# mLSTM scores and sums as three rounded products, with the values' remainders in DRAM

## The chip, the cores and the metric

The kernel runs on one core of one Trainium2 chip. The metric is the time of one execution in microseconds (us) on the device. Its engines are named as in the profile: PE is TensorE (PEld its weight loads), DVE VectorE, ACT ScalarE, POOL GpSimd, SP SyncE, which issues most of the DMAs.

## The reference

One decoder layer on 512 tokens of width 1024, in float32. An mLSTM with four heads (queries and keys of 128, values of 256) and a windowed attention run beside each other on one normalised input; sigmoid gates merge them; an output projection, a squared-ReLU MLP and a gated embedding follow.

```python
qk_ml = jax.nn.silu(causal_depthwise_conv(qk_ml, conv_qk[i]))
q_ml, k_ml = jnp.split(qk_ml, 2, axis=-1)
...
# mLSTM, chunkwise; over the whole sequence a head computes
scores = jnp.einsum("bhtk,bhsk->bhts", qc, kc) * jnp.exp(log_d - m_t[..., None])
num = (... + jnp.einsum("bhts,bhsv->bhtv", scores, vc))
den = ... + jnp.sum(scores, axis=-1)
h = num / jnp.maximum(jnp.abs(den), jnp.exp(-m_t))[..., None]
...
y_a = jax.nn.sigmoid(o_ml) * h_ml          # h_ml: h normalised per head
y_b = swa_with_sinks(...)                  # the local branch
merged = jax.nn.sigmoid(g_a) * (y_a @ w_branch_a[i]) + jax.nn.sigmoid(g_b) * (y_b @ w_branch_b[i])
x = x + merged @ w_out[i]
u = rmsnorm(x, norm_mlp_g[i]) @ w_up[i]
x = x + jnp.square(jax.nn.relu(u)) @ w_down[i]
```

## The kernel before, in words

All 512 tokens stay on the chip. A projection is made of rounded products: each float32 operand is split (`split`) into a high part, rounded to the type fp32r by a ScalarE copy, and a low part, what VectorE's subtraction leaves of it. `pairs` names the three products high x high, high x low and low x high, which `chain` adds up in one PSUM bank. Weights go through `load_w`: SP loads 512 KB into a `wr` tile, ScalarE casts it to `wh`, VectorE makes `wl`. `split_by_transfer` makes a low part in another way: ScalarE writes the negated high part, and an accumulating DMA from POOL's queue adds the source (its rows are at L147).

The stages that the change touches come in this order. First `by_tokens(w_vml, ...)`: the values, with `seven`, which forms the product of two 2 x 2 block matrices from seven block products, named p1, c11, t21, t22, c22, c12 and c21 after what becomes of them. The function `post` takes each from PSUM: p1 is copied, the t are p1 plus a product, and the c go to `put_v`, which writes a token tile of values `vm[m]` (all heads, 257 columns each, the last one ones, so that the sums over scores come out of the same matmul). Then the mLSTM's gates, rows of 4 x 512 (`mst`, the running maximum; `rr`; `gg`; `em`), TensorE's transposes of gg and em, and `by_tokens(w_o, ...)`, the output gate, with its own p1 to c21. Then the gates of the branches, the conv, and the local branch's attention.

Last comes the stage of the heads. `ml_decay(h)` makes a head's decay weights with ten exps into four tiles `dm`. `ml_scores(h)` multiplies keys and queries (float32 matmuls, four blocks, the causal part alone) and VectorE multiplies the decay in. `ml_out(h)` sums them over values: ten float32 matmuls in two PSUM tiles. `ml_norm` normalises, `branch_b(i)` is one of eight projections of the local branch (24 products of 512 columns), `ya_of(h)` transposes a head's result and splits it into the two big tiles `ya`, and `merge` projects those.

The order of instructions on each engine isn't that of the program text: a scheduler places them ahead of time by its own estimate of durations, and `issue_after` gives it limits. Tiles come from pools of numbered buffers, and a new tile waits until the last reader of the buffer's tile before it is through. The pool `act` has `NACT` = 34 buffers of 128 x 512, and nearly every short-lived tile lives in it; `lm` has four buffers of 128 x 1024, `big` two of 8 x 512 columns. PSUM has two buffers each of `psg` and `pst` (one bank) and of `psa` (two banks).

Of the kernel before, what the change touches and what calls it, by code (L numbers as in the profile page):

```python
# [22 lines left out]
NEG = -1e30  # L23
NH = 4
DV = 256
# [7 lines left out]
LMB = 4  # L33
# [3 lines left out]
def block_kernel(  # L37
# [29 lines left out]
    nc = tc.nc  # L67
    V, A, G, T = nc.vector, nc.scalar, nc.gpsimd, nc.tensor
# [18 lines left out]
    def nm(s):  # L87
        n_names[0] += 1
        return f"{s}_{n_names[0]}"
# [16 lines left out]
    def act_f(n="f"):  # L106
        return ap.tile([P, 512], F32, tag="act", bufs=NACT, name=nm(n))

    def act_r(n="r"):
        return ap.tile([P, 512], F32R, tag="act", bufs=NACT, name=nm(n))  # L110
# [4 lines left out]
    def big_hl(n):  # L115

        hl = [bp.tile([P, KT, 512], F32R, tag="big", bufs=2, name=nm(n)) for _ in range(2)]
        return hl, [[t[:, k, :] for t in hl] for k in range(KT)]

    def tk(n):  # L120
        return tp_.tile([P, NH * (DV + 1)], F32, tag="tk", bufs=4, name=nm(n))

    def tok_scratch(n="lm"):
        return sp.tile([P, D], F32, tag="lm", bufs=LMB, name=nm(n))
# [4 lines left out]
    def r32(t):  # L129
        return t.bitcast(F32)  # L130
# [3 lines left out]
    def split(dst, src, scale=None):  # L134

        if scale is None:
            A.copy(dst[0], src)  # L137
            last_low[0] = V.tensor_sub(dst[1], src, r32(dst[0]))  # L138
        else:
            A.activation(dst[0], src, AF.Copy, scale=scale)  # L140
            V.scalar_tensor_tensor(dst[1], src, scale, r32(dst[0]), ALU.mult, ALU.subtract)
# [21 lines left out]
    def pairs(a, b):  # L163

        return [(a[0], b[0]), (a[0], b[1]), (a[1], b[0])]

    last_mm = [None]
# [36 lines left out]
    ones = cp.tile([P, P], F32, name="ones")  # L204
# [129 lines left out]
    on_scalar, _ = columns(0, xn)  # L334
# [4 lines left out]
    _, on_vector = columns(1, xn)  # L339
    for m in range(NT):  # L340
        if m == 1:
            with tc.issue_after(on_vector):
                xn, _ = norm(2)
# [17 lines left out]
    dp = pool(ctx, "dp", space=bass.MemoryType.DRAM)  # L361
# [3 lines left out]
    with tc.issue_after(gate_in.ins):  # L365
        hi, lo = [r32(t[:, :, :P]) for t in h2]
# [37 lines left out]
    for i in range(2):  # L404
        ps = proj_T(w_ksw, i, ps_t)
        both = [act_r("kk"), act_r("kk")]
        low = [act_r("kl"), act_r("kl")]
        for ab in range(2):
            s, o = HALF[ab], HALF[1 - ab]
# [67 lines left out]

    vm = []
    for m in range(NT):
        t = tk("vm").rearrange("p (h d) -> p h d", h=NH)  # L480
        G.memset(t[:, :, DV : DV + 1], 1.0)
        vm.append(t)

    def by_tokens(w, post, own_first=False):

# [30 lines left out]

    def put_v(m, nh, ps, k):
        o = vm[m][:, 2 * nh : 2 * nh + 2, :DV]
        src = ps.rearrange("p (h d) -> p h d", h=2)
        if k is None:  # L520
            A.copy(o, src)
        else:
            V.tensor_add(o, src, k.rearrange("p (h d) -> p h d", h=2))

    pg = ps_a()
    pgi, pgf = pg[:, :512], pg[:, 512:]
# [134 lines left out]
    qk = [None] * 8  # L661
# [113 lines left out]
    for h in range(NH):  # L775
        silu(h)
        silu(4 + h)


    hs = [[act_f("hs") for _ in range(2)] for _ in range(NH)]  # L780
    hd = c1.tile([P, NH, NT], F32, name="hd")
    hss = c1.tile([P, NH, NT], F32, name="hss")
    wts = {}
# [4 lines left out]
    def ml_decay(h):  # L788
        pr = rows[h]
        dg = act_f("dg")  # L790
        V.tensor_tensor(
            dg.rearrange("p (t j) -> p t j", t=NT),
            pr.rearrange("p (t j) -> p t j", t=NT),
            tri.unsqueeze(1).broadcast_to([P, NT, P]),
            ALU.add,
        )
        wT = []
        for s in range(NT):
            dm = act_f("dm")
            for t in range(s, NT):  # L800
                src = dg if t == s else pr
                A.activation(
                    dm[:, t * P : (t + 1) * P],
                    src[:, t * P : (t + 1) * P],
                    AF.Exp,
                    bias=gc[:, t * NT + s, h : h + 1],
                )
            wT.append(dm)
        wts[h] = wT

    def ml_scores(h):

        two, one = ps_a(), ps_t()
        banks = [two[:, :512], two[:, 512:], one, two[:, 512:]]
        at = [0, 0, 0, 384]
        for s in (0, 1, 3, 2):
            n0 = s * P
            psc = banks[s][:, at[s] : at[s] + S - n0]
            T.matmul(psc, qk[4 + h][:, n0 : n0 + P], qk[h][:, n0:], start=True, stop=True, skip_group_check=True)  # L819
        for s in range(NT):  # L820
            n0 = s * P
            dm = wts[h][s]
            V.tensor_mul(dm[:, n0:], banks[s][:, at[s] : at[s] + S - n0], dm[:, n0:])

    def ml_out(h):
        wT = wts.pop(h)
        for half in (1, 0):
            pn = ps_a().rearrange("p (n c) -> p n c", n=2)
            for t in (2 * half, 2 * half + 1):
                for s in range(t + 1):  # L830
                    last_mm[0] = T.matmul(  # L831
                        pn[:, t % 2, : DV + 1], wT[s][:, t * P : (t + 1) * P], vm[s][:, h, :], start=s == 0, stop=s == t, skip_group_check=True
                    )
            A.copy(hs[h][half].rearrange("p (n c) -> p n c", n=2), pn[:, :, :DV])
            V.tensor_copy(hd[:, h, 2 * half : 2 * half + 2], pn[:, :, DV])
        den = small("den", NT, 2)
        V.scalar_tensor_tensor(den, hd[:, h, :], -1.0, hd[:, h, :], ALU.mult, ALU.max)
        V.tensor_max(den, den, gc[:, NT * NT :, h])
        rd = small("rd", NT, 3)
        V.reciprocal(rd, den)  # L840
        jk = act_f("jk")
        for t in range(NT):
            A.activation(jk[:, :DV], h_of(h, t), AF.Square, scale=rd[:, t : t + 1], accum_out=hss[:, h, t : t + 1])
        return rd
# [15 lines left out]
    def branch_b(i):  # L860
        ps = ps_g()
        mm_T(ps, load_w(w_b[i], KT * P, KT), yb)
        t2[i] = act_f("gb")
        V.tensor_mul(t2[i], ps, gate_of(gbd, i))


    _, ya = big_hl("ya")

    def ya_of(h):
        for i in (2 * h, 2 * h + 1):  # L870
            pt = ps_t()
# [2 lines left out]
            split(ya[i], pt, gml[:, i : i + 1])  # L874

    ml_decay(0)
    ml_scores(0)
    rds = []
    for h in range(NH):
        branch_b(h)  # L880
        if h + 1 < NH:
            ml_decay(h + 1)
        with tc.issue_after(last_mm[0].ins):
            rds.append(ml_out(h))
        if h + 1 < NH:
            with tc.issue_after(last_mm[0].ins):
                ml_scores(h + 1)
        if h == 1:
            ml_norm([0, 1], rds)
        elif h > 1:  # L890
            ml_norm([h], rds[h:])
    for h in range(NH):
        branch_b(NH + h)
        ya_of(h)


    F11, F12, F22, G1, G2, G3, G4 = ([] for _ in range(7))

# [96 lines left out]
    _, x1 = big_hl("x1")  # L995
# [273 lines left out]
    def one(n):  # L1269
        return tp.tile([P, 1], F32, tag=n, bufs=4, name=nm(n))  # L1270
# [48 lines left out]
    for m in range(NT):  # L1319
        for o, n in ((0, 512),) if m == 0 else ((0, 256), (256, 256)):  # L1320
            ps = ps_g()[:, :n]
# [4 lines left out]
            if o == 0:  # L1326
                s = one("fse")
# [102 lines left out]
```

## Time and profile before

| what | value |
|---|---|
| median of 3 runs (lowest to highest) | 881.58 us (881.02 to 881.89) |
| the profiled execution's own time | 881.1 us |
| its span | 879.3 us |
| busy: PE, DVE, ACT, POOL | 99%, 75%, 55%, 3% |
| mean granted clock of TensorE | 0.997 |
| DMA moved | 105.16 MB, 120 GB/s |
| stage of the values, first to last product | about 47 to 82 us |
| output gate | about 83 to 126 us |
| stage of the heads, first projection of the local branch to the first merge | 325.4 to 399.5 us |

The span is the time that the profile covers; 1.8 us of the profiled execution's time lie outside it. Rows of the timeline give the start and the duration of an instruction in us; matmuls are pipelined, so the distance from one start to the next says what a matmul takes, not its duration. A float32 matmul shows as two records.

### The profile page before, as it was taken

To read this page: it belongs to the slowest core of one execution; us is meant where nothing else is said; L and a number is where in the kernel's file an instruction comes from. 1 tells how busy PE (TensorE), PEld (TensorE's weight loads), DVE (VectorE), ACT (ScalarE), POOL (GpSimd) and SP (SyncE) were. 2 spreads that over 40 slices of the span, in tenths; PEclk is the share of its full clock that TensorE was granted. 3 is DMA by queue.
4 is the path that set the end of the run, shared out by engine and by line. 5 is a ranking of instruction groups with operands and counts; after the bars stand their busy time and mean duration, and the time that the engine had idled before them with its cause. 6 is when DMAs were issued, how large, how long until landed. Compare 5 with 4: busy or idle time off the path is not lost.

```text
span 879.3 us, 11531 instructions
## 1 busy us (share of the span) xinstructions
PE 866.8 (99%) x4372; PEld 725.4 (82%) x4372; DVE 661.1 (75%) x972; ACT 481.0 (55%) x799; POOL 28.8 (3%) x52
## 2 busy tenths in 40 slices
PE   8999999999999999999999999999999999999996
PEld 7888889998777777888888888888888888887886
DVE  6999887875789876665896669757956784699557
ACT  6684554544675768743344665356435534544843
POOL 1111010000000000000020000000000000000000
PEclk9999999999999999999999999999999999999998
DMA  7765244435122162364244612530452054102402
GB/s 266 211 188 176 73 152 165 166 115 195 49 73 72 49 202 85 99 238 144 72 82 148 226 48 72 203 108 2 140 172 72 1 191 144 48 25 75 142 0 96
DMA packets 31929, 105.16 MB, mean 120 GB/s; under 512 B 4477, under 2 KB 4477, under 8 KB 31874
## 3 DMA queue, kind: packets, MB, share of 16 engines
q1 hardware_dynamic: 27570, 93.15, 30.6%
q0 software_dynamic: 4160, 11.02, 4.8%
q8 instruction: 34, 0.56, 0.3%
q10 hardware_dynamic: 144, 0.26, 0.1%
q14 instruction: 21, 0.17, 0.1%
HBM read 91.30 MB, written 8.40 MB: 113 GB/s over the span
## 4 chain that ended last, share of the span: by engine, by line
PE 89%; DVE 4%; ACT 3%; DMA 2%; issue 1%; SPq 0%; ACTq 0%; DVEq 0%
PE psg L171 49%; PE psp L171 23%; PE psa L171 7%; PE pst L171 4%; PE psa L831 1%; PE pst L747 1%; DVE wl L138 1%; DMA wr<-in_w_vsif 1%; ACT lm L712 1%; PE psa L819 1%; PE psa L689 1%; PE psa L690 1%; ACT wh L137 0%; DMA wr<-in_w_gb 0%; PE psp L980 0%
## 5 line engine op out<-in xcount | busy, mean ns | idle before, releaser
L137 ACT CAST wh<-wr 128x1024 fp32r<-128x1024 f32 x138 | 144.8, 1052 | 181.6 <-PE psg L171 71.7
L138 DVE TENSOR_TENSOR wl<-wr,wh 128x1024 fp32r<-128x1024 f32 x138 | 167.6, 1220 | 83.7 <-ACT wh L137 82.5
L171 PE MATMUL psg<-x,wh 128*128 128x512 f32 x512 | 157.7, 389 | 0.0
L171 PE MATMUL psp<-wh,uf 128*128 128x512 f32 x448 | 138.6, 389 | 0.0
L171 PEld LDWEIGHTS psg<-x,wh 128*128 128x128 f32 x512 | 96.0, 188 | 19.9
L171 PE MATMUL psg<-x,wl 128*128 128x512 f32 x256 | 99.6, 389 | 0.0
L171 PEld LDWEIGHTS psp<-wh,uf 128*128 128x128 f32 x448 | 84.1, 188 | 17.4
L171 PE MATMUL psp<-wl,uf 128*128 128x512 f32 x224 | 87.3, 390 | 0.8 <-DVE wl L138 0.8
L171 PE MATMUL psg<-h,wh 128*128 128x512 f32 x256 | 81.1, 395 | 0.7 <-DVE rc L715 0.7
L137 ACT CAST wh<-wd 128x1024 fp32r<-128x1024 f32 x44 | 46.2, 1053 | 56.4 <-PE psp L171 21.9
L138 DVE TENSOR_TENSOR wl<-wd,wh 128x1024 fp32r<-128x1024 f32 x44 | 53.2, 1220 | 14.6 <-ACT wh L137 14.5
L171 PEld LDWEIGHTS psg<-x,wl 128*128 128x128 f32 x256 | 48.0, 188 | 10.0
L171 PEld LDWEIGHTS psg<-h,wh 128*128 128x128 f32 x256 | 47.0, 188 | 11.2 <-issue 1.6
L171 PE MATMUL psg<-h,wl 128*128 128x512 f32 x128 | 50.5, 395 | 0.0
L171 PEld LDWEIGHTS psp<-wl,uf 128*128 128x128 f32 x224 | 42.0, 188 | 10.0 <-DVE wl L138 1.2
L138 DVE TENSOR_TENSOR uf<-F,uf 128x1792 fp32r<-128x1792 f32 (+2 forms) x20 | 33.0, 1652 | 21.8 <-ACT uf L137 21.8
L171 PE MATMUL psg<-yb,wh 128*128 128x512 f32 x128 | 41.3, 402 | 0.1
L171 PE MATMUL psg<-ya,wh 128*128 128x512 f32 x128 | 39.5, 390 | 0.0
L137 ACT CAST uf<-F 128x1792 fp32r<-128x1792 f32 (+2 forms) x20 | 27.9, 1396 | 20.6 <-DVE F L1133 20.4
L1157 DVE SCALAR_TENSOR_TENSOR xk<-psp,r,xk 128x512 f32<-128x512 f32 x48 | 33.8, 745 | 4.9 <-PE psp L171 4.7
L171 PE MATMUL psa<-h,wh 128*128 128x256 f32 x192 | 35.3, 285 | 0.3 <-ACT p L625 0.3
L171 PE MATMUL psg<-hS,wh 128*128 128x256 f32 x192 | 35.6, 284 | 0.0
(321 smaller groups left out, 1742.1 us busy)
## 6 DMA issues: line engine op xcount, KB each, us to landing
wr<-in_w_up SPq DMA_DIRECT2D x32, 512.0 KB, 3.2
wd<-in_w_down SPq DMA_DIRECT2D x24, 512.0 KB, 3.6
wr<-in_w_qsw SPq DMA_DIRECT2D x8, 512.0 KB, 3.7
gd<-gr POOLq DMA_DIRECT2D x8, 512.0 KB, 3.5
wr<-in_w_qkml SPq DMA_DIRECT2D x8, 512.0 KB, 3.2
wr<-in_w_b SPq DMA_DIRECT2D x8, 512.0 KB, 3.2
gl<-gd SPq DMA_DIRECT2D x8, 512.0 KB, 3.2
wr<-in_w_a SPq DMA_DIRECT2D x8, 512.0 KB, 4.1
```

The costliest lines, as they stand in the source:

```text
L137: A.copy(dst[0], src)
L138: last_low[0] = V.tensor_sub(dst[1], src, r32(dst[0]))
L171: last_mm[0] = T.matmul(ps, l, r, start=first and i == 0, stop=last and i == len(ops) - 1, skip_group_check=parts)
L689: T.matmul(o, q[:, n * P : (n + 1) * P], kk[kp][ab][:, k0 : k0 + 256], start=True, stop=False)
L690: T.matmul(o, q[:, n * P : (n + 1) * P], kl[kp][ab][:, k0 : k0 + 256], start=False, stop=True)
L712: A.activation(lm3[:, g, :], lm3[:, g, :], AF.Exp, bias=nmx[:, g : g + 1], scale=0.125, accum_out=sm[:, g : g + 1])
L747: T.matmul(o[HALF[ab], :], v[:, c : c + 64], w[:, ab * 512 : (ab + 1) * 512], start=j == 0, stop=j == len(terms) - 1)
L819: T.matmul(psc, qk[4 + h][:, n0 : n0 + P], qk[h][:, n0:], start=True, stop=True, skip_group_check=True)
L831: last_mm[0] = T.matmul(pn[:, t % 2, : DV + 1], wT[s][:, t * P : (t + 1) * P], vm[s][:, h, :], start=s == 0, stop=s == t, skip_group_check ...
L1157: pin(V.scalar_tensor_tensor(o, ps[:, t, :], r2[:, 2 * toks + t : 2 * toks + t + 1], o, ALU.mult, ALU.add))
```

## The change

What it does:

- `put_v` keeps the values' high parts in `vm` (now fp32r, 258 columns a head, the last two ones, written by ScalarE in place of POOL's memset) and makes a remainder `vl` of each of eight half tiles: two by VectorE's subtraction, six by a negated copy on ScalarE and an accumulating DMA. POOL stores all eight in DRAM (`vld`).
- `ml_out` reads a head's remainders back (SP, an `lm` buffer) and makes each of ten sums from three rounded products.
- `qk_parts` splits a head's queries and keys, `ml_scores` makes each block from three rounded products and splits the weighted scores; the parts lie in the big tiles `ya`, which are taken earlier. A head has three `dm` tiles instead of four.
- Six of the eight `branch_b` stand among the heads (one, two, two, one), two after them; before, four and four.

```diff
@@ -477,9 +477,10 @@
 
     vm = []
     for m in range(NT):
-        t = tk("vm").rearrange("p (h d) -> p h d", h=NH)
-        G.memset(t[:, :, DV : DV + 1], 1.0)
+        t = tp_.tile([P, NH * (DV + 2)], F32R, tag="tk", bufs=4, name=nm("vm")).rearrange("p (h d) -> p h d", h=NH)
+        A.copy(t[:, :, DV:], ones[:, : 2 * NH].rearrange("p (h d) -> p h d", h=NH))
         vm.append(t)
+    vld = dp.tile([P, NH, NT, DV], F32, name="vld")
 
     def by_tokens(w, post, own_first=False):
 
@@ -516,11 +517,17 @@
 
     def put_v(m, nh, ps, k):
         o = vm[m][:, 2 * nh : 2 * nh + 2, :DV]
-        src = ps.rearrange("p (h d) -> p h d", h=2)
+        two = lambda t: t.rearrange("p (h d) -> p h d", h=2)
+        low = act_r("vl")
         if k is None:
-            A.copy(o, src)
+            A.copy(o, two(ps))
+            V.tensor_sub(two(low), two(ps), r32(o))
         else:
-            V.tensor_add(o, src, k.rearrange("p (h d) -> p h d", h=2))
+            V.tensor_add(k, ps, k)
+            A.copy(o, two(k))
+            A.activation(low, k, AF.Copy, scale=-1.0)
+            nc.gpsimd.dma_start(out=r32(low), in_=k, accum_op=ALU.add)
+        nc.gpsimd.dma_start(out=vld[:, 2 * nh : 2 * nh + 2, m, :], in_=two(r32(low)))
 
     pg = ps_a()
     pgi, pgf = pg[:, :512], pg[:, 512:]
@@ -776,6 +783,21 @@
         silu(h)
         silu(4 + h)
 
+    ya_parts, ya = big_hl("ya")
+
+    turn = [0]
+
+    def spare():
+
+        k = turn[0] % KT
+        turn[0] += 1
+        return [t[:, k, :] for t in ya_parts]
+
+    def qk_parts(h):
+        for i in (h, 4 + h):
+            hl = spare()
+            split(hl, qk[i])
+            qk[i] = hl
 
     hs = [[act_f("hs") for _ in range(2)] for _ in range(NH)]
     hd = c1.tile([P, NH, NT], F32, name="hd")
@@ -794,43 +816,51 @@
             tri.unsqueeze(1).broadcast_to([P, NT, P]),
             ALU.add,
         )
-        wT = []
+        dm = [act_f("dm") for _ in range(3)]
+        wT = [dm[0], dm[1][:, :384], dm[2][:, :256], dm[2][:, 256:384]]
         for s in range(NT):
-            dm = act_f("dm")
             for t in range(s, NT):
                 src = dg if t == s else pr
                 A.activation(
-                    dm[:, t * P : (t + 1) * P],
+                    wT[s][:, (t - s) * P : (t - s + 1) * P],
                     src[:, t * P : (t + 1) * P],
                     AF.Exp,
                     bias=gc[:, t * NT + s, h : h + 1],
                 )
-            wT.append(dm)
-        wts[h] = wT
+        wts[h] = dm, wT
 
     def ml_scores(h):
 
         two, one = ps_a(), ps_t()
-        banks = [two[:, :512], two[:, 512:], one, two[:, 512:]]
-        at = [0, 0, 0, 384]
-        for s in (0, 1, 3, 2):
-            n0 = s * P
-            psc = banks[s][:, at[s] : at[s] + S - n0]
-            T.matmul(psc, qk[4 + h][:, n0 : n0 + P], qk[h][:, n0:], start=True, stop=True, skip_group_check=True)
+        psc = [two[:, :512], two[:, 512:896], one[:, :256], one[:, 256:]]
+        q, k = qk[h], qk[4 + h]
         for s in range(NT):
-            n0 = s * P
-            dm = wts[h][s]
-            V.tensor_mul(dm[:, n0:], banks[s][:, at[s] : at[s] + S - n0], dm[:, n0:])
+            n0 = min(s, 2) * P
+            ops = pairs([t[:, s * P : (s + 1) * P] for t in k], [t[:, n0:] for t in q])
+            for j, (l, r) in enumerate(ops):
+                T.matmul(psc[s], l, r, start=j == 0, stop=j == 2, skip_group_check=True)
+        dm, wT = wts[h]
+        hl = []
+        for j, n in enumerate((512, 384, 384)):
+            for s in ((0,), (1,), (2, 3))[j]:
+                V.tensor_mul(wT[s], psc[s][:, P:] if s == 3 else psc[s], wT[s])
+            hl.append([t[:, :n] for t in spare()])
+            split(hl[j], dm[j][:, :n])
+        wts[h] = hl + [[t[:, 256:] for t in hl[2]]]
 
     def ml_out(h):
         wT = wts.pop(h)
+        low = sp.tile([P, NT, DV], F32R, tag="lm", bufs=LMB, name=nm("vl"))
+        nc.sync.dma_start(out=r32(low), in_=vld[:, h])
         for half in (1, 0):
             pn = ps_a().rearrange("p (n c) -> p n c", n=2)
             for t in (2 * half, 2 * half + 1):
                 for s in range(t + 1):
-                    last_mm[0] = T.matmul(
-                        pn[:, t % 2, : DV + 1], wT[s][:, t * P : (t + 1) * P], vm[s][:, h, :], start=s == 0, stop=s == t, skip_group_check=True
-                    )
+                    hi, lo = [q[:, (t - s) * P : (t - s + 1) * P] for q in wT[s]]
+                    o = pn[:, t % 2, : DV + 2]
+                    T.matmul(o, hi, vm[s][:, h, :], start=s == 0, stop=False, skip_group_check=True)
+                    T.matmul(o[:, :DV], hi, low[:, s, :], start=False, stop=False, skip_group_check=True)
+                    last_mm[0] = T.matmul(o, lo, vm[s][:, h, :], start=False, stop=s == t, skip_group_check=True)
             A.copy(hs[h][half].rearrange("p (n c) -> p n c", n=2), pn[:, :, :DV])
             V.tensor_copy(hd[:, h, 2 * half : 2 * half + 2], pn[:, :, DV])
         den = small("den", NT, 2)
...
     ml_decay(0)
+    qk_parts(0)
     ml_scores(0)
     rds = []
+    todo = list(range(KT))
     for h in range(NH):
-        branch_b(h)
+        branch_b(todo.pop(0))
         if h + 1 < NH:
             ml_decay(h + 1)
+            qk_parts(h + 1)
         with tc.issue_after(last_mm[0].ins):
             rds.append(ml_out(h))
         if h + 1 < NH:
+            if h:
+                branch_b(todo.pop(0))
             with tc.issue_after(last_mm[0].ins):
                 ml_scores(h + 1)
         if h == 1:
@@ -890,9 +923,9 @@
         elif h > 1:
             ml_norm([h], rds[h:])
     for h in range(NH):
-        branch_b(NH + h)
+        if h % 2 == 0:
+            branch_b(todo.pop(0))
         ya_of(h)
```

Where it moves instructions. POOL's queue from the last tiles of `hS` (split by transfer) to the gate's row `rrd` and the first store of the output gate, before:

```order
L147 DMA hS_125_657<-s4_118_640 128x512
L147 DMA hS_127_662<-s4_118_640 128x512
L554 DMA rrd_864<-rr_157_862 4x512
L565 DMA row_163_879<-rrd_864 128x512
L565 DMA row_164_880<-rrd_864 128x512
L565 DMA row_165_881<-rrd_864 128x512
L565 DMA row_166_882<-rrd_864 128x512
L590 DMA god_907<-sgo_190_1001 128x2x256
```

And now, from the first of the six accumulations to `rrd`; `vl_146` and `vl_147` belong to c22, `vl_152` and `vl_153` to c12, `vl_158` and `vl_159` to c21:

```order
L529 DMA vl_146_783<-t22_140_747 128x512
L529 DMA vl_147_789<-t22_141_749 128x512
L530 DMA vld_538<-vl_146_783 128x2x256
L529 DMA vl_152_827<-p1_112_601 128x512
L530 DMA vld_538<-vl_147_789 128x2x256
L529 DMA vl_153_833<-p1_113_603 128x512
L530 DMA vld_538<-vl_152_827 128x2x256
L530 DMA vld_538<-vl_153_833 128x2x256
L529 DMA vl_158_871<-t21_134_711 128x512
L529 DMA vl_159_877<-t21_135_713 128x512
L530 DMA vld_538<-vl_158_871 128x2x256
L561 DMA rrd_901<-rr_165_899 4x512
```

Six accumulations and their stores, each behind its accumulation, now stand ahead of `rrd` (the last store just behind it); before, nothing stood between `hS` and `rrd`.

TensorE at the end of the values (`psa_103` is c21's tile), before; `pst_176` is the output gate's p1:

```order
L171 MATMUL psa_103_563<-wl_151_829,h_16_158 128x512
L171 MATMUL psa_103_563<-wh_150_828,h_17_159 128x512
L572 MATMUL psa_94_538<-ident_80,gg_158_866 128x4
L574 MATMUL psa_94_538<-ident_80,em_162_877 128x4
L572 MATMUL psa_94_538<-ident_80,gg_159_867 128x4 x2
L574 MATMUL psa_94_538<-ident_80,em_162_877 128x4
...
L171 MATMUL pst_176_925<-wh_180_929,h_16_158 128x512
```

And now; p1 (`pst_184` and `pst_185`) goes on between the second row and the third:

```order
L171 MATMUL psa_103_564<-wh_156_855,h_17_159 128x512
L171 MATMUL pst_184_962<-wh_188_966,h_16_158 128x512
...
L171 MATMUL pst_185_963<-wh_190_982,h_17_159 128x512
L171 MATMUL psg_186_964<-wh_200_1045,hS_60_387 128x512
L579 MATMUL psa_94_539<-ident_80,gg_166_903 128x4
L171 MATMUL psg_187_965<-wh_200_1045,hS_60_387 128x512
L581 MATMUL psa_94_539<-ident_80,em_170_914 128x4
L579 MATMUL psa_94_539<-ident_80,gg_167_904 128x4 x2
...
L171 MATMUL pst_184_962<-wh_194_1006,h_16_158 128x512
```

The transposes of gg and em have moved from ahead of the output gate's p1 to behind it; the first matmuls of its t21 (`psg`) stand among them, and c11 (`pst_184` from `wh_194`) comes after.

ScalarE at the start of the heads, from the last silu (`sg`) to the first exps (`dm`), before:

```order
L675 ACTIVATE sg_597_3384<-acc_589_3358 128x512
L137 COPY wh_690_3786<-wr_689_3784 128x1024
L802 ACT_TABLE_LOAD
L802 ACTIVATE dm_609_3401<-row_163_879,gc_901 128x128
L802 ACTIVATE dm_609_3401<-dg_608_3399,gc_901 128x128
L802 ACTIVATE dm_609_3401<-row_163_879,gc_901 128x128 x2
```

And now, and then from head 0's last exp on; `ya_606` holds high parts, first of four queries and keys of heads 0 and 1, then of the weighted scores:

```order
L682 ACTIVATE sg_605_3421<-acc_597_3395 128x512
L137 COPY ya_606_3424<-acc_380_2375 128x512
L137 COPY ya_606_3424<-acc_484_2843 128x512
L137 COPY ya_606_3424<-acc_501_2933 128x512
L137 COPY ya_606_3424<-acc_533_3057 128x512
L137 COPY wh_684_3885<-wr_683_3883 128x1024
L824 ACT_TABLE_LOAD
L824 ACTIVATE dm_617_3438<-row_171_916,gc_938 128x128
L824 ACTIVATE dm_617_3438<-dg_616_3436,gc_938 128x128
L824 ACTIVATE dm_617_3438<-row_171_916,gc_938 128x128 x2
...
L824 ACTIVATE dm_619_3440<-dg_616_3436,gc_938 128x128
L137 COPY ya_606_3424<-dm_617_3438 128x512
L137 COPY ya_606_3424<-dm_618_3439 128x384
L137 COPY wh_695_3955<-wr_694_3953 128x1024
```

Four copies have come ahead of the weight's cast and the exps' table load, and a head's exps are followed by the copies of its weighted scores.

More of the change, by code (lines that the diff above doesn't have):

```diff
@@ L120, in tk @@
     def tk(n):
-        return tp_.tile([P, NH * (DV + 1)], F32, tag="tk", bufs=4, name=nm(n))
+        return tp_.tile([P, NH * (DV + 2)], F32, tag="tk", bufs=4, name=nm(n))
     def tok_scratch(n="lm"):
@@ L864, in branch_b @@
         V.tensor_mul(t2[i], ps, gate_of(gbd, i))
-    _, ya = big_hl("ya")
     def ya_of(h):
```

## The prediction

> **What bounds the kernel now.** I read the page's busy times and its chain first, then the list of what TensorE waits for over the whole span.
>
> ```profile
> PE 866.8 (99%) x4372; PEld 725.4 (82%) x4372; DVE 661.1 (75%) x972; ACT 481.0 (55%) x799; POOL 28.8 (3%) x52
> ...
> PE 89%; DVE 4%; ACT 3%; DMA 2%; issue 1%; SPq 0%; ACTq 0%; DVEq 0%
> ...
> PE psa L311 <- ACT xn L296: 1.2, 1, 1.2
> ...
> PE psp L171 <- DVE wl L138: 0.8, 1, 0.8
> ```
>
> TensorE is busy for 866.8 of 879.3 us and makes 89% of the chain. Its longest wait is 1.2 us, in the first stage; after that none passes 0.8. So the program is one row of matmuls: time taken out of TensorE's row is gained, and a new pause in it is lost, since no stage behind has idle time that could take it up. The question is what the change takes out, and whether its splits, copies and DMAs hold TensorE up anywhere. Sums go from the profiled execution's own 881.1 us, 0.5 below the median of 881.58.
>
> **Matmul work: -3.4 us.** These are TensorE's rows in the timeline: a projection of the local branch (three products of 512 columns from one row to the next), two rounded products of 256 columns, 8 of 10 sums of a head (two records each), and one head's scores, with what follows them.
>
> ```profile
> 327.46 0.62 PE L171 MATMUL psg<-yb,wh 128*128 128x512 f32 x2
> 327.91 0.39 PE L171 MATMUL psg<-yb,wl 128*128 128x512 f32 x1
> 328.14 0.62 PE L171 MATMUL psg<-yb,wh 128*128 128x512 f32 x2
> ...
> 302.05 0.28 PE L689 MATMUL psa<-kk,qs 128*128 128x256 f32 x1
> 302.17 0.28 PE L690 MATMUL psa<-kl,qs 128*128 128x256 f32 x1
> ...
> 340.29 3.63 PE L831 MATMUL psa<-vm,dm 128*128 128x257 f32 x16
> 343.75 0.59 PE L819 MATMUL pst<-acc,acc 128*128 128x256 f32 x2
> 344.19 1.89 PE L819 MATMUL psa<-acc,acc 128*128 128x512 f32 x6
> 345.83 0.48 PE L171 MATMUL psg<-yb,wl 128*128 128x512 f32 x1
> ```
>
> Three products of 512 take 0.68, so one takes 0.227; one of 256 takes 0.12; for 384 I take the value between, 0.173. Before, a head's scores take 345.83 - 343.75 = 2.08, and its sums (343.75 - 340.29) / 16 x 20 = 4.33. After, scores are three products each of 512, 384, 256 and 256 columns (the last is widened by a block): 3 x (0.227 + 0.173 + 0.12 + 0.12) = 1.92. Sums are 30 products of 256 or 258 columns: 30 x 0.121 = 3.63. That is 6.41 against 5.55: 0.86 a head, 3.4 for four. The eight projections are the same work in another order.
>
> **A new wait at the start of the o gate's products: +5.1 us.** put_v now writes a remainder for each half of the values. Two of eight come from VectorE alone, six by a negated copy on ScalarE, an accumulating DMA and a store, all from POOL's queue. The remainder's buffers, and those of the sums they are taken from, belong to the pool "act", and the gate tiles mst, rr, gg, em and the o gate's p1 are the next to take them. By the order, mst now stands behind a store, rr and gg behind accumulations and stores, and the table load ahead of em behind the last accumulation (vl_159). The p1 copies stand on ScalarE behind em, and TensorE's transposes of gg and em now stand after the o gate's first product, ahead of the one that needs p1. Rows of that place before, TensorE, ScalarE and VectorE:
>
> ```profile
> 82.09 0.39 PE L171 MATMUL psa<-wh,h 128*128 128x512 f32 x1
> 82.41 0.22 PE L572 MATMUL psa<-ident,gg 4*128 4x4 f32 x1
> ...
> 83.37 0.50 PE L171 MATMUL pst<-wh,h 128*128 128x512 f32 x1
> ...
> 78.16 1.28 ACT L562 ACT_TABLE_LOAD   x1
> 79.54 0.63 ACT L562 ACTIVATE em<-mst 4x512 f32<-4x512 f32 x1
> ...
> 87.84 0.59 ACT L507 COPY p<-pst 128x512 f32<-128x512 f32 x1 [0.32 <-PE pst L171]
> ...
> 83.37 1.27 DVE L523 TENSOR_TENSOR vm<-psa,t 128x512 f32<-128x512 f32 x2
> ```
>
> Before, em is ready at 80.1 and the transposes follow the values' last product without a pause. Prices of the DMAs come from those of the same size and kind: POOL's issue rows of an accumulation and of a store, then time to landing, for accumulations over the kernel, for the four near this place, and for two stores.
>
> ```profile
> 51.78 0.84 POOL L147 DMA_DIRECT2D hS<-s  x1 [1.89 <-ACT hS L146]
> 52.82 0.85 POOL L147 DMA_DIRECT2D hS<-s  x1 [0.20 <-issue]
> ...
> 94.12 0.72 POOL L590 DMA_DIRECT2D god<-sgo  x1 [13.05 <-ACT sgo L586]
> ...
> DMA to landing us min/median/max: 3.2/4.4/6.4
> ...
> hS<-s POOLq DMA_DIRECT2D x4, 256.0 KB, 3.9
> ...
> god<-sgo POOLq DMA_DIRECT2D x2, 256.0 KB, 2.5
> ```
>
> POOL takes them in order, and a store waits for its accumulation to land. The third one (vl_153) goes out at about 81.9, after the stores ahead of it. It lands at 81.9 + 3.9 = 85.8; its store holds POOL to 86.5, the accumulation of vl_158 to 87.55 (pitch 1.04), and vl_159 goes out then. The data for it are ready by 87.05: adds to about 85.4 (84.64 in the row above; weight work that now stands ahead makes it some 0.8 later, an estimate), then copies and negated copies at 0.55. It lands at 87.55 + 3.9 = 91.45; the table load (1.28) and em (0.55, the pitch of such rows) end at 93.3. TensorE, which has left out the transposes, is through with p1's 24 products (24 x 0.227 = 5.45) and two more at 82.32 + 5.9 = 88.2, and stands still to 93.3. Transposes take another 0.85 beside the p1 copy; the next product starts at 94.15 instead of 82.32 + 5.45 + 0.45 + 0.85 = 89.05: 5.1 later. At the low end (the remainder's accumulation goes out at 84.9, straight after its data, and lands in 3.2) the next product starts at 90.8: 1.7 later. With landings of 6.4 for one of the two in the chain it is 7.6. I take the rows near the place. [...]
>
> Earlier in that stage ScalarE gets 12 copies of 0.55 more and VectorE two of 0.64; TensorE's margins there are some tenths, so 0 to +0.4; I take 0.
>
> **The clock in that pause: +1.0 us.** TensorE's last matmul of the kernel and the granted clock (the column behind POOL) behind it:
>
> ```profile
> 871.96 0.28 PE L171 MATMUL psg<-wh,x 128*128 128x256 f32 x1
> ...
> 872.24:874.00 1.76, 0.00 (x0) 0.00 (x0) 1.15 (x3) 1.71 (x2) 0.00 (x0) 1.00 0.78 298
> 874.00:874.50 0.50, 0.00 (x0) 0.00 (x0) 0.23 (x3) 0.25 (x2) 0.00 (x0) 0.82 0.00 0
> 874.50:879.30 4.80, 0.00 (x0) 0.00 (x0) 0.88 (x2) 0.72 (x1) 0.00 (x0) 0.50 0.28 109
> ```
>
> 0.82 over half a microsecond puts the fall to 0.50 at 874.3, 2.1 us after the last matmul. A pause of 5.1 us passes that, and products behind it start at half speed. No row shows how long; if the rise takes as long as the fall, 2.1 us at half speed lose 1.0. The bounds are 0 (no fall) and 2.5 (half speed for as long as the pause).
>
> **Inside the head stage: +2.4 and +0.4 us.** Head 0's weights now need exps, product and split before the first sum. ScalarE's rows before, and TensorE's start on head 0's sums:
>
> ```profile
> 331.39 1.66 ACT L675 ACTIVATE sg<-acc 128x512 f32<-128x512 f32 x3
> 332.95 1.04 ACT L137 CAST wh<-wr 128x1024 fp32r<-128x1024 f32 x1
> 334.01 1.28 ACT L802 ACT_TABLE_LOAD   x1
> 335.31 0.40 ACT L802 ACTIVATE dm<-row,gc 128x128 f32<-128x128 f32 x1
> ...
> 338.23 0.39 ACT L802 ACTIVATE dm<-dg,gc 128x128 f32<-128x128 f32 x1
> 338.96 1.03 PE L831 MATMUL psa<-vm,dm 128*128 128x257 f32 x4
> ```
>
> Four copies of q and k (four at 0.55, the pitch of the three rows of sg) now stand ahead of the 1024-wide cast: 332.95 + 2.2 + 1.04 + 1.28 and ten exps (335.31 to 338.6, 3.15 without a gap) end at 340.6, and the copy of the first weights at 341.15. TensorE has done both projections and the scores by 338.7 to 338.8, and the next projection can't fill: it needs one of two psg buffers, whose reader stands on VectorE behind the weights' products. So 2.4 us, between 0 (the exps end as before) and 3.5 (one more split late). Heads 1 to 3 have a projection between scores and sums, longer than their splits: 0.
>
> At the end, VectorE's subtraction of w_out's quarters now stands ahead of heads' norm and waits for a load:
>
> ```profile
> wo<-in_w_out SPq DMA_DIRECT2D x4, 512.0 KB, 4.4
> ```
>
> It is issued when the last sums end; with 4.4 to landing, head 3's tiles come 0.4 late for their transposes (0 to 1.5).
>
> The sum: 881.1 + 5.1 + 1.0 - 3.4 + 2.4 + 0.4 = 886.6 us.
>
> **The rivals.** A difference of 0.2% (1.8 us) is about what a measurement of this kernel tells from none; measured from 881.58, the limits are 879.8 and 883.3.
>
> 1. *The removed matmuls are the whole effect* (faster). It needs the last accumulation to land by 86.4, so that em is there when TensorE is, and head 0's exps to end as before. For it: TensorE is the bound, and POOL is idle for 97%. Against: by 86.4 the data for that DMA are hardly there. It gives 881.1 - 3.4 = 877.7. Chance 0.07. With the DMA's wait gone but head 0's left, 881.1 - 3.4 + 2.8 = 880.5: chance 0.10.
> 2. *The DMA's wait is at its low end*: 881.1 + 1.7 - 0.6 = 882.2, to 883.5 with landings between; a pause of 2 us leaves the clock as it is. For it: the first accumulation of the four landed in 3.2. Chance 0.13.
> 3. *The clock comes back late.* As a mechanism of this kernel, from the rows: the pause passes the 2.1 us after which the clock fell, and half speed lasts for as long as the pause did, so 2.5 us are lost instead of 1.0, and the time is 888.1; with the same at head 0's pause of 2.4 us, also past 2.1, 889.3. For it: the fall is in the trace. Against: no row shows a rise, and a pause of 2.4 is close to the limit. Chance 0.20. [...]
>
> The forecast, both waits near the values taken, has 0.50: 884 to 888.
>
> **How the numbers follow.** 886.6 is the likeliest case. Left out of the range are rival 1 in both forms (0.17) and a little above 890, so it reaches from 881.5 to 890. Faster by over 0.2%: 0.07 of rival 1 and 0.01 for errors elsewhere, 0.08. Within: 0.10 of it and half of rival 2, 0.16. Slower: 0.76.
>
> **What the profile after would show.** Right: TensorE's list of waits has one of about 5 us at the transposes of gg and em, near 88 us, with the clock under 1 behind it; ScalarE idles before its table load there until an accumulation lands; and one of about 2.4 at head 0's first sums. Scores take 1.9 and sums 3.6 a head. Wrong: no wait over 1 us at 88; transposes straight after p1; a head's sums over 4 us; or time lost after 405 us, where the order is as before.

## The result and the profile after

The changed kernel takes 892.13 us (median of 4 runs, 891.70 to 892.97), the kernel before in the same comparison 881.32: a ratio of 1.0125 (95% interval 1.0113 to 1.0137), 10.8 us slower. The profiled execution of the changed kernel took 892.97 us, 11.9 above that of before. The prediction of 886.6 us had the direction and the two places, but the time lies above its range.

The page of the changed kernel, its busy times and its chain:

```profile
PE 869.7 (98%) x4428; PEld 730.6 (82%) x4428; DVE 672.9 (76%) x994; ACT 497.2 (56%) x835; POOL 39.9 (4%) x62
...
PE 83%; DVE 6%; ACT 5%; DMA 3%; issue 2%; SPq 0%; POOL 0%; ACTq 0%; DVEq 0%; POOLq 0%
```

TensorE's share of the chain has fallen from 89% to 83%, and its busy time has risen by 2.9 us although its matmuls are worth less: part of them ran at a lower clock. The waits in its list that before did not have (what waited, for whom, total us, times, longest):

```profile
PE psa L581 <- ACT em L569: 3.0, 1, 3.0
PE psg L171 <- ACT wh L137: 2.6, 1, 2.6
PE psa L861 <- ACT ya L137: 2.1, 1, 2.1
PE psa L579 <- DVE gg L565: 1.1, 1, 1.1
...
PE pst L901 <- DVE ya L141: 0.5, 1, 0.5
```

Three lie at the start of the output gate, one at head 0's first sums, one at head 3's transposes. TensorE's rows around the first three, then the first product of c11 and the first one behind it:

```profile
88.05 0.39 PE L171 MATMUL pst<-wh,h 128*128 128x512 f32 x1
91.00 0.50 PE L171 MATMUL psg<-wh,hS 128*128 128x512 f32 x1 [2.56 <-ACT wh L137]
92.62 0.22 PE L579 MATMUL psa<-ident,gg 4*128 4x4 f32 x1 [1.12 <-DVE gg L565]
...
96.29 0.27 PE L581 MATMUL psa<-ident,em 4*128 4x4 f32 x1 [3.02 <-ACT em L569]
...
97.77 0.80 PE L171 MATMUL pst<-wh,h 128*128 128x512 f32 x1
...
106.04 0.39 PE L171 MATMUL psg<-wl,hS 128*128 128x512 f32 x1
```

Between 88.3 and 97.8 TensorE does two products and 14 transposes. Then c11 takes 106.04 - 97.77 = 8.3 us for 24 products, which take 24 x 0.227 = 5.45 by the rows of before, where the clock was 1.00. Stretches of the span say why (busy times of PE, PEld, DVE, ACT and POOL, then the granted clock, the DMA share and GB/s):

```profile
88.20:93.30 5.10, 1.40 (x5) 0.51 (x3) 5.10 (x10) 3.69 (x6) 2.78 (x4) 1.00 0.71 181
93.30:93.40 0.10, 0.00 (x0) 0.00 (x0) 0.10 (x2) 0.00 (x0) 0.10 (x1) 0.69 1.11 205
93.40:103.50 10.10, 7.21 (x27) 5.94 (x28) 5.58 (x12) 3.25 (x5) 3.84 (x7) 0.50 0.50 164
103.50:103.60 0.10, 0.10 (x2) 0.10 (x1) 0.00 (x0) 0.10 (x1) 0.00 (x0) 0.61 0.00 0
...
352.70:352.80 0.10, 0.10 (x3) 0.07 (x1) 0.10 (x1) 0.10 (x1) 0.00 (x0) 0.75 1.21 492
352.80:356.10 3.30, 3.30 (x16) 3.14 (x15) 3.26 (x7) 2.84 (x8) 0.00 (x0) 0.50 0.16 66
356.10:356.20 0.10, 0.10 (x3) 0.10 (x2) 0.10 (x1) 0.10 (x1) 0.00 (x0) 0.69 0.00 0
```

TensorE ran at half its clock for 10.2 us here and for 3.4 us behind head 0's wait. By where TensorE reaches the same products in both kernels, the loss is +0.5 us at the end of the values' products (82.84 instead of 82.09 + 0.23 = 82.32), +11.3 at the output gate's first product of 256 columns (135.77 instead of 124.46), still +11.2 at the local branch's first projection, and +11.9 from 414 us to the last matmul.

How the pauses came about, on ScalarE:

```profile
81.96 0.63 ACT L528 ACTIVATE vl<-p 128x512 fp32r<-128x512 f32 x1 [3.26 <-DMA vl<-t]
82.50 1.03 ACT L137 CAST wh<-wr 128x1024 fp32r<-128x1024 f32 x1
...
94.31 1.28 ACT L569 ACT_TABLE_LOAD   x1 [2.42 <-DMA vl<-t]
95.61 0.63 ACT L569 ACTIVATE em<-mst 4x512 f32<-4x512 f32 x1
```

On POOL's queue:

```profile
76.07 1.89 POOL L529 DMA_DIRECT2D vl<-t  x2 [17.07 <-ACT vl L528]
82.16 0.75 POOL L530 DMA_DIRECT2D vld<-vl  x1 [4.20 <-DMA vl<-t]
...
89.50 1.83 POOL L529 DMA_DIRECT2D vl<-t  x2
```

And on VectorE; the last fence is the row of the first two accumulations among the DMA issues (KB each, median us to landing):

```profile
83.56 1.23 DVE L138 TENSOR_TENSOR wl<-wr,wh 128x1024 fp32r<-128x1024 f32 x1 [2.66 <-ACT wh L137]
...
87.10 1.28 DVE L526 TENSOR_TENSOR t<-psa,t 128x512 f32<-128x512 f32 x2
```

```profile
vl<-t POOLq DMA_DIRECT2D x2, 256.0 KB, 5.9
```

The first two accumulations (issued from 76.07) landed in 5.9 us. Until then not only the stores stood: ScalarE's negated copy for `vl_152` waited 3.26 us for one of them. Its tile takes a buffer that the accumulation still used; as the store of the first remainder goes out only at 82.16, behind that copy, this must be the buffer of an accumulation's source. Behind that copy on ScalarE stood the cast of the output gate's weights, behind the cast VectorE's split (idle for 2.66), and behind the splits the adds for c21 (87.10). So the last two accumulations went out at 89.5 to 91.3, the table load ahead of em came at 94.31, and em at 95.61.

### The profile page after: what moved, and what is told of

The parts are those of the page before. It is cut to its first block, busy times and chain, and to the rows that moved or that the text cites. A ratio compares the mean times of both kernels' runs of the same rounds, so it can differ in the third digit from the quotient of the medians.

```text
span 891.2 us, 11712 instructions
## 1 busy us (share of the span) xinstructions
PE 869.7 (98%) x4428; PEld 730.6 (82%) x4428; DVE 672.9 (76%) x994; ACT 497.2 (56%) x835; POOL 39.9 (4%) x62
## 4 chain that ended last, share of the span: by engine, by line
PE 83%; DVE 6%; ACT 5%; DMA 3%; issue 2%; SPq 0%; POOL 0%; ACTq 0%; DVEq 0%; POOLq 0%
PE psg L171 46%; PE psp L171 22%; PE psa L171 6%; PE pst L171 2%; DVE wl L138 2%; PE pst L754 1%; ACT wh L137 1%; DMA vl<-t 1%; DMA xt<-in_x 1%; DMA wq<-in_w_o 1%; ACT lm L719 1%; PE psa L863 1%; PE psa L861 1%; PE psa L696 1%; PE psa L862 1%
```

## The experiments

**What the DMAs are worth.** The six accumulations and eight stores are left out; the order on the engines stays, and the sums read another buffer of DRAM of the same shape.

```diff
             A.activation(low, k, AF.Copy, scale=-1.0)
-            nc.gpsimd.dma_start(out=r32(low), in_=k, accum_op=ALU.add)
-        nc.gpsimd.dma_start(out=vld[:, 2 * nh : 2 * nh + 2, m, :], in_=two(r32(low)))
```

> The changed kernel with the six accumulating DMAs and the eight stores of the values' remainders left out; the sums read the output gate's store instead, of the same size, so the sums use wrong remainders. All copies, negated copies and subtractions stay, and every engine but POOL and SP has its instructions in the same order. My theory (the gate tiles wait for buffers that these DMAs hold, and the long pause halves the clock): no wait over 1 us near 88, no fall of the clock there, and the 11.3 us that the values and the output gate lost shrink to about 0.5; 892.1 - 10.8 = 881.3, to 882.5. Rival one (ScalarE's twelve extra copies, and the transposes' place behind p1, make the pause): it stays, 889 to 892. Rival two (the traffic delays the weights' loads): the wait goes but so do delays all over the stage; that is told by the places.

It took 884.98 us, 1.0048 of before (1.0033 to 1.0063): between the theories. TensorE's waits, and the stretch at half speed:

```profile
PE psa L858 <- ACT ya L137: 2.1, 1, 2.1
PE psa L578 <- ACT em L566: 1.6, 1, 1.6
...
PE psa L576 <- DVE gg L562: 0.6, 1, 0.6
```

```profile
92.80:96.10 3.30, 3.30 (x9) 2.65 (x8) 3.30 (x6) 0.00 (x0) 0.72 (x2) 0.50 0.86 264
```

At the output gate's products of 256 columns it is 4.8 us behind before (129.24), not 11.3. So 6.5 of the 11.3 need the DMAs. The other 4.8 come with what this kernel keeps, the twelve more copies on ScalarE and the new order: the gates' rows and em stand behind the values' copies and the weights' casts, TensorE still pauses for gg and em, and the clock still halves for 3.4 us. Copies and order were not told apart.

**Either half of the change alone.** First the heads' part with before's values, again with sums that read another buffer:

```diff
-        low = act_r("vl")
...
-            V.tensor_add(k, ps, k)
-            A.copy(o, two(k))
...
+            V.tensor_add(o, two(ps), two(k))
...
-        nc.sync.dma_start(out=r32(low), in_=vld[:, h])
+        nc.sync.dma_start(out=r32(low), in_=god[:, h])
```

> The changed heads alone: values as before (one add each into the rounded tile, no remainders made or stored); the sums read the output gate's store as the remainder, of the same size. Leaves out the values' remainders. My theory: the values' stage is as before, the heads lose 2.1 at head 0, 1.7 to the clock behind it, 0.5 at the end, and gain 3.4: 881.3 + 0.7 = 882.0 (881 to 883). Rival (the heads' waits come from the shift and the traffic of the earlier stage and go with it): 881.3 - 3.4 = 877.9.

881.38 us, 1.0003 (0.9994 to 1.0013): nothing is left of the 3.4 us. The wait at head 0 is there, and half speed behind it:

```profile
PE psa L854 <- ACT ya L137: 2.1, 1, 2.1
```

```profile
341.60:344.90 3.30, 3.30 (x17) 3.27 (x16) 3.26 (x7) 2.83 (x8) 0.00 (x0) 0.50 0.25 98
```

Then the values' part alone: the kernel before with `put_v`, `vm` and `vld` of the changed one, and sums that read `vm` as they did. Against before, beside those lines:

```diff
-                        pn[:, t % 2, : DV + 1], wT[s][:, t * P : (t + 1) * P], vm[s][:, h, :], start=s == 0, stop=s == t, skip_group_check=True
+                        pn[:, t % 2, : DV + 1], wT[s][:, t * P : (t + 1) * P], r32(vm[s][:, h, : DV + 1]), start=s == 0, stop=s == t, skip_group_check=True
```

> The values' part alone: before's heads with float32 matmuls, the values' high parts rounded, their remainders made and stored as in the changed kernel but never read (the sums leave the remainders out). My theory: the stage loses its 11.3 whatever the heads do; 881.0 + 11.3 = 892.3 (891 to 893.5), the heads as before. Rival (a later stage has slack that takes some of it back): under 890.

892.13 us, 1.0123 (1.0109 to 1.0137), the median of the changed kernel itself. So the stage of the values carries the whole loss, and the heads' part comes out at nothing beside it too.

**The clock.** To keep TensorE busy while em is late, needless products of 512 columns are put between the output gate's p1 and the transposes, 32 in one kernel and 40 in the other (`gate_columns` holds the transposes of gg and em). The first two products of t21, which the changed kernel does between its pauses, come later.

```diff
+                with tc.issue_after(last_mm[0].ins):
+                    for i in range(FILL):
+                        mm = T.matmul(Z[0], hT[0][0][:, :P], hT[0][0], start=True, stop=True, skip_group_check=True)
+                gate_columns(mm.ins)
```

> The changed kernel with 32 needless matmuls of 512 columns (7.3 us) on TensorE in the pause at 88 us, ahead of the transposes, into a PSUM bank that t21 overwrites. Nothing else moves but t21's first matmuls. Clock theory: TensorE is at work when its granted clock would fall, so c11 runs at 0.227 a matmul instead of 0.35 to 0.43: 892.1 - 3.3 = 888.8. Rival (c11 is slow because its weights come late, or the clock falls whatever TensorE does): 892 or, if the needless work is in the way, more.

> As fill, with 40 needless matmuls, 9.1 us, so that the pause is filled to about 97.4. Clock theory: no fall of the clock from 88 to 110, c11's 24 products take 5.45 us instead of 8.3 (after) and about 6.6 (fill); 1.7 less than fill's 894.0 where em comes no later: 892.3. Rival: the clock falls near 98 with TensorE at work, c11 takes over 6.

With 32 it took 893.96 us (1.0142, 1.0125 to 1.0159), with 40 it took 891.42 (1.0117, 1.0101 to 1.0133). A row of TensorE and a stretch of the kernel with 32, then the same of that with 40, show the main reason why more needless work was quicker by 2.5 us:

```profile
97.74 0.22 PE L594 MATMUL psa<-ident,em 4*128 4x4 f32 x1 [1.90 <-ACT em L579]
```

```profile
98.90:102.20 3.30, 3.30 (x9) 2.52 (x9) 2.26 (x7) 0.00 (x0) 0.00 (x0) 0.50 0.68 230
```

```profile
88.28 9.23 PE L505 MATMUL psg<-h 128*128 128x512 f32 x40
97.44 0.22 PE L592 MATMUL psa<-ident,gg 4*128 4x4 f32 x1
```

```profile
96.00:108.00 12.00, 12.00 (x63) 9.85 (x62) 6.93 (x12) 7.45 (x10) 3.15 (x6) 1.00 0.51 175
```

32 products ended before em was there; a pause of 1.90 us was left, and the clock halved behind it, so the first of the two kernels missed its expectation. Part of that is the edit's own: em came at 97.05 instead of 95.61, since the table load ahead of it now waited for the landing of a store, to 95.76. With 40 no pause is left, the clock stays at 1.00, and c11 takes 5.6 us (98.40 to 103.97) instead of 8.3, so late weights were not what slowed it. It ends 1.85 us earlier than with 32 (105.82); most of the other 0.7 is a wait for a copy `p` among the products of 256 columns, 0.5 us instead of 1.2. Against the changed kernel, c11 starts 0.6 us later, and the products of 256 columns start 1.6 earlier (134.19). That is about the clock's loss in c11 (2.8 us) less the late start and the two products of t21 (0.45); the accumulations and stores are the same.

**Remainders without accumulating DMAs.** First all by VectorE, each pair in one `pT` buffer instead of two of `act`:

```diff
-            A.activation(low, k, AF.Copy, scale=-1.0)
-            nc.gpsimd.dma_start(out=r32(low), in_=k, accum_op=ALU.add)
+            V.tensor_sub(two(low), two(k), r32(o))
```

> The changed kernel with all remainders made by VectorE's subtraction (six more of 512 columns, no accumulating DMA, no negated copies) into tiles of the pool pT, idle in this stage, and stored from there. All of the computation is there. My theory: act's buffers come free as before; 892.1 - 11.3 + 0.5 = 881.3 to 882.5, no wait over 1 us near 88. Rival (any way of making the remainders is too much for this stage, since VectorE is busy for 96% of it from 40 to 70 us): waits for wl on TensorE of 1 us and more, 884 to 888.

883.41 us, 1.0021 (1.0012 to 1.0030), slightly above what was expected. The transposes stand behind c21 again, no wait over 0.3 us is left at em, and the clock stays at 1.00. VectorE is now the limit there (the third busy time):

```profile
PE psa L171 <- ACT p L638: 0.8, 3, 0.4
...
PE psa L587 <- ACT em L575: 0.3, 1, 0.3
```

```profile
80.00:104.00 24.00, 23.21 (x110) 18.30 (x109) 23.98 (x35) 14.87 (x18) 6.47 (x10) 1.00 0.56 185
```

It is 2.1 us behind before at the products of 256 columns (126.53). Then the same with POOL doing the six subtractions (`G.tensor_sub`):

> The changed kernel with six remainders made by a subtraction on POOL (idle there) into tiles of pT, in place of negated copies and accumulating DMAs; all of the computation is there. My theory (dve_rest's remaining 2.1 us in the stage are VectorE's six extra subtractions): with VectorE relieved, 0.5 to 1.0 remains of the values' stage; 881.2 - 0.2 (heads, from head_alone) + 0.8 = 881.8 (881.0 to 882.5). Rival (POOL's subtractions slow VectorE's beside them, or the stage's loss is ScalarE's copies): 883 and more.

890.63 us, 1.0108 (1.0092 to 1.0124): the theory that an idle POOL does this for nothing fell. TensorE's longest wait, and rows of POOL, ScalarE and VectorE:

```profile
PE psa L587 <- ACT em L575: 6.2, 1, 6.2
```

```profile
75.36 2.05 POOL L535 TENSOR_TENSOR vl<-t,vm 128x512 fp32r<-128x512 f32 x1 [16.37 <-ACT vm L534]
...
78.46 1.21 POOL L535 TENSOR_TENSOR vl<-t,vm 128x512 fp32r<-128x512 f32 x1
...
84.63 4.02 POOL L535 TENSOR_TENSOR vl<-p,vm 128x512 fp32r<-128x512 f32 x1
...
88.68 0.63 ACT L575 ACTIVATE em<-mst 4x512 f32<-4x512 f32 x1 [3.23 <-POOL vl L535]
...
76.28 1.68 DVE L564 TENSOR_TENSOR rr<-fl,mst 4x512 f32<-4x512 f32 x1
```

Subtractions of one size took 2.05, 1.21 and 4.02 us, and em waited for the longest. VectorE's `rr` took 1.68 us beside the first of them; in the changed kernel, without POOL's work, it takes 0.67. What made `rr` and the longest subtraction slower than the others was not shown.

**Head 0.** The queries and keys of head 1 are split only after head 0's exps, in the changed kernel otherwise as it is:

```diff
+    first_exps = last_exp[0].ins
...
-            qk_parts(h + 1)
+            with tc.issue_after(first_exps) if h == 0 else ExitStack():
+                qk_parts(h + 1)
```

> The changed kernel; only the splits of head 1's queries and keys are held behind head 0's exps. My theory (head 0's first sum waits for exps that stand behind four copies of 0.55): the pause of 2.1 us shrinks by 1.1 to about 1.0, too short for the clock to fall; 892.1 - 1.1 = 891.0, and 889.3 where the clock had fallen. Rival (the exps wait for the cast or the table load, whatever stands ahead): 2.1 as before, 892.1.

890.33 us, 1.0103 (1.0085 to 1.0121), 1.8 below the changed kernel's median. The wait has another name and is shorter, and the clock stays at 1.00 from 338 to 360 us:

```profile
PE psg L171 <- DVE gb L896: 1.4, 1, 1.4
```

```profile
338.00:360.00 22.00, 20.43 (x110) 17.20 (x109) 20.18 (x40) 21.41 (x48) 0.00 (x0) 1.00 0.31 107
```

With this edit, POOL's subtractions and the subtraction of w_out's quarters held behind the last of `ya`:

> pool_rest, with head 1's splits held behind head 0's exps and the subtraction of w_out's quarters held behind the last split of the heads' results. My theory: 881.8 less 1.1 at head 0 (and less the clock's 1.7 where it fell), less 0.5 to 1.3 at the end: 879.6 (878.5 to 880.6), faster than both kernels. Rival (TensorE finds the next wait and the gain of the matmuls goes into that): 881 to 882.

889.40 us, 1.0094 (1.0078 to 1.0110), a miss by 10 us for the reason above: em's wait of 6.2 us is the same.

**Mended.** Two remainders (c21's) by accumulation as in the changed kernel, the others by VectorE; the head 0 edit; w_out's subtraction later; and a projection of the local branch ahead of head 0's scores:

```diff
+            if nh == 0 and m < 2:
+                A.activation(low, k, AF.Copy, scale=-1.0)
+                nc.gpsimd.dma_start(out=r32(low), in_=k, accum_op=ALU.add)
+            else:
+                V.tensor_sub(two(low), two(k), r32(o))
...
+    branch_b(todo.pop(0))
     ml_scores(0)
...
+            with tc.issue_after(last_ya):
+                V.tensor_sub(b, b_out[3][j - 1], b)
```

> All of the computation, mended in four places: values' remainders by VectorE's subtraction into pT, but c21's two by negated copy and accumulating DMA (as in the changed kernel, into pT); head 1's splits behind head 0's exps; the first projection of the local branch written ahead of the scores, so that VectorE frees its psg buffer early and a third projection can fill head 0's pause; w_out's subtraction behind the last split of the heads. My theory (what is lost beside the matmuls' gain of 3.4 is waits, and each has its place): dve_rest's 883.4, less 2.1 to 2.6 at head 0, less 0.5 at the end, less about 1 of VectorE's two subtractions: 879.5 (878.5 to 880.8). Rival (the values' stage is bound by VectorE and keeps its 2 us, the heads find other waits): 881 to 883.

880.31 us, within the range expected; the ratio is 0.9997 (0.9989 to 1.0006), no difference from before. Eight of its runs lie between 879.95 and 881.2, three between 882.5 and 883.1. The same edits of the heads with before's values, as in the kernel with the heads' part alone, show what the heads can give:

> head_alone with the three mends in the heads (head 1's splits later, the first projection's product early, w_out's subtraction later); leaves out the values' remainders, as head_alone. My theory (the matmul work saved is 3.4 and comes through when nothing waits): 881.0 - 3.4 + 0.3 = 877.9 (877.3 to 879). Rival (the saving is less than the rows of the trace make it, since splits on ScalarE and VectorE hold TensorE up in many small waits): 879.5 to 881.

879.34 us, 0.9979 (0.9970 to 0.9988). That is 2.0 us better than the heads' part without the edits, but above the range expected: not all of the 3.4 of the matmuls comes through. Of the new waits these are left:

```profile
PE psg L172 <- DVE gb L890: 1.0, 1, 1.0
...
PE pst L897 <- DVE ya L142: 0.3, 1, 0.3
```

With them 3.5 - 1.0 - 0.3 = 2.2 should be saved; its last matmul starts 2.1 earlier than that of before (869.87 against 871.96).

## Why the prediction was wrong, step by step

- *Matmul work, -3.4*: right. In the changed kernel, the first rows of a head's scores and sums and of what follows them:

```profile
385.06 0.28 PE L841 MATMUL pst<-ya 128*128 128x256 f32 x1
...
386.98 0.62 PE L171 MATMUL psg<-yb,wh 128*128 128x512 f32 x2
...
392.45 0.28 PE L861 MATMUL psa<-vm,ya 128*128 128x258 f32 x1
...
396.06 0.62 PE L171 MATMUL psg<-yb,wh 128*128 128x512 f32 x2
```

  Scores take 1.92 us and sums 3.61: 0.88 a head less than before, 3.5 for four.
- *Wait at the o gate, +5.1*: right in place and mechanism, wrong in size. c11 starts at 97.77 instead of 89.05 + 0.5 (the values' products ended 0.5 late) = 89.6: 8.2 us, above the bound of 7.6; of it about 0.6 is that the transposes run at half clock (97.77 - 96.29 = 1.5 instead of 0.85). Two sub-steps failed. The landing of 3.9 us held for the later accumulations (3.2 to 3.6), but the first pair took 5.9. And the step "the data for it are ready by 87.05" counted VectorE's and ScalarE's work without a wait among it. The negated copy of `vl_152` waited 3.26 us for a landing, with the o gate's casts queued behind it, so VectorE's adds ended at 88.4 instead of 85.4, and the last accumulation landed by 94.3 instead of 91.45. The working looked for tiles of the gate that wait for a buffer of the remainders or their sources, not for remainders that do.
- *The clock in that pause, +1.0*: the step that the rise takes as long as the fall failed, and with it the reading of the fall as a delay of 2.1 us: the clock stayed at 1.00 through the first wait of 2.56, and at the end of the changed kernel it fell 4.5 us after the last matmul (884.14 to 888.64). Half speed lasted 10.2 us and cost 2.8 in c11 and 0.6 in the transposes, 3.4 together.
- *Head 0, +2.4*: the wait was 2.1. Half speed behind it, which the sum left out and a rival held, cost another 1.7 (half of 3.4).
- *The end of the heads, +0.4*: 0.5.

The terms as measured: 0.5 + 7.6 + 3.4 - 3.5 + 2.1 + 1.7 + 0.5 = 12.3, against 11.9 by the profiled executions. The wait was 2.5 and the clock 4.1 us larger than in the sum (the latter counted at both places). The rival nearest to the result was the clock that comes back late, with head 0's pause as well, at 889.3: what it names, half speed behind both pauses, is in the traces, and the two fills and the head 0 edit support it. Its measure is not: half speed did not last as long as the pause (10.2 us with waits of 6.7 in all, 3.4 with 2.1), and it kept the wait at 5.1. The rival that the removed matmuls are the whole effect is out in both its forms: even without the DMAs the kernel took 885.0 us, not 877.7 or 880.5.

Two things stay open. Why the first pair of accumulations took 5.9 us and later ones 3.2 to 3.6 was not separated (the 3.2 to 6.4 that the prediction quotes for accumulations before holds both); loads of 512 KB for the output gate were under way beside them, but no run took those away. And how much of the 6.5 us of the DMAs is the late negated copy and how much the late last landing was not told apart, since leaving the DMAs out removes both.

## What to carry to other kernels

Before a remainder is moved to an accumulating DMA, list for each of its buffers, and for its source, which instruction takes the buffer next and what is queued behind that instruction on its engine: here a 256 KB DMA held ScalarE for 3.26 us, ScalarE held weight casts, and these held VectorE (idle for 2.66 us) and the next DMA. In this kernel, where TensorE is the bound, the pause of 2.12 us at head 0 cost about 1.7 more where the clock was at 0.50 for 3.4 us behind it, so a fix that shortens a pause or fills it with real matmuls is worth counting with the clock. Here the pause in the first head, which has nothing to stand between its scores and its sums, and the clock behind it took back all that the matmuls of four heads saved.

## What the runs showed of the hardware that was not expected

Half speed came in pieces of one length. With the edges taken from the clock in 0.1 us stretches, the changed kernel was at half speed from 93.34 to 103.58 (10.24 us) and from 352.75 to 356.16 (3.41 us): three times 3.41 and once, and the two falls are 259.41 us apart, 76 times 3.413. The kernel without DMAs and the one with 32 needless products have stretches of 3.41 us as well, the one with POOL's subtractions one of 6.83, twice that.

The same pause did not always have half speed behind it. The pause at head 0 in the kernel without DMAs, and the stretch around it:

```profile
345.65 0.39 PE L858 MATMUL psa<-vm,ya 128*128 128x258 f32 x1 [2.12 <-ACT ya L137]
```

```profile
336.00:360.00 24.00, 21.88 (x131) 19.38 (x130) 20.23 (x40) 23.41 (x61) 0.00 (x0) 1.00 0.28 89
```

The pause is 2.12 us here, in the changed kernel, in the one with VectorE's remainders and in the one with the heads' part alone. The clock stayed at 1.00 here and with VectorE's remainders; it halved for 3.4 us in the other two. The author's estimate of where the pause lies counts steps of 259.41 / 76 = 3.413 us from a fall of the same trace. In the changed kernel the whole pause (350.1 to 352.2) lies within the step that ended at 352.75, which leaves 1.3 us of work in it; in the kernel without DMAs, counted on from the fall at 92.75, it lies across an edge, with 1.6 of work in the first of the two steps.

Other kernels with this pause (2.08 to 2.12 us) agree. Where the clock halved (the heads' part alone at 341.59, 32 needless products at 354.85, 40 at 351.46), the whole pause lies in the step before the fall, with 1.3 us of work left. With POOL's subtractions, where it did not, an edge counted from their fall at 87.19 lies inside the pause, at 350.0, with 2.0 us of work before it.

So at head 0 a step with 1.3 us of work ended in a fall and one with 1.6 did not, and by this count whether the pause of 2.1 us cost 1.7 more went with where it fell. The prediction's 2.1 us fit this too: the 3.41 us that ended at the fall at 874.3 held 1.3 us of work. No limit follows from it: with 32 needless products the 3.41 us ahead of the fall at 98.85 held 1.5 us of work, and without DMAs those ahead of the fall at 92.75 held 1.8, both with transposes of gg and em among it. That the clock goes by such steps is the author's reading of these distances; no run shifted a pause by itself. Nor was it shown whether the two groups of the mended kernel's runs, some 2 us apart, come from this: only one of those runs has a trace.
